# Staging of weights in a two-block fp32-accurate kernel: host-packed units of one transfer each, issued by SyncE instead of ScalarE

## Chip, cores and metric

One Trainium2 chip, one core. The metric is device time in microseconds of one execution. A trace of one execution of the kernel before is read below; "PE" is TensorE, "DVE" VectorE, "ACT" ScalarE, "POOL" GpSimd, "SP" SyncE, and a "q" behind an engine's name (ACTq, SPq) is that engine's instruction queue, where transfers are issued.

## What is computed

Two blocks of layers on 512 tokens of 1,024 features, in float32. The first block has two layers, each with three mixers that run side by side (sparse attention over the top 128 keys, gated linear attention, a pooling mixer) and a feed-forward network with a short convolution. The second block has four layers (kinds A, B, C, A): grouped attention, neighbourhood attention, differential attention, with a context stream of 256 tokens beside the 512.

```python
x = first_block(x, positions, norm1_g, w_in, ..., w_out, norm2_g, w_up, conv_w, conv_b, w_down, final_norm_g)
...
h = rms_norm_2(x, norm_g[i]) * (1.0 + sc[:, None]) + sh[:, None]
u, z = jnp.split(h @ w_in, [n_mix_cols], axis=-1)
...
x = x + gt[:, None] * ((o * jax.nn.silu(z)) @ w_out)
```

What matters here is the products with weights: `w_in`, `w_out`, `w_up`, `w_down` in the first block and three pairs of `w_in`, `w_out` in the second, all float32 in HBM.

## The kernel before, in words

Every weight goes through a staging unit. `wsplit` (L303) takes a tile `wst` of 128 x 1024 float32 (four buffers), begins its transfers on ScalarE's queue (L311), and makes two float16 halves of 256 times the weight: `whi`, the rounded value, by ScalarE (L322, or L318 and L319 in the first block's mixers), and `wlo`, the rest, by VectorE (L323) or GpSimd (L320). `whi` and `wlo` have four buffers each. TensorE then does three products for each block of 128 rows (L338 to L340 and L1564 to L1566). A buffer of `wst` is free again when `wlo` has been made, so up to four units are staged and four are split ahead of TensorE.

The transfers read the weights as they lie in HBM: a unit of eight row blocks by 128 columns is one transfer whose rows are 512 bytes long; a pair unit of the second block (`pair_job`, L1547) is two such transfers, one for each chunk of columns; a unit of `early1` and `late1` is two transfers of 1 KB rows; a unit of an output matrix of the second block is one transfer of 2 KB rows. The first unit of each mixer layer (`unit` with parts, L761) holds three narrow pieces of 16, 4 and 64 columns: VectorE clears the tile and three transfers fill it.

SyncE's queue has the other transfers: the input `xin` (L246), the modulation weights `ast` (L414), copies of heads between partitions (`put_q`, `put_k`, L606 to L615; `swap_heads`, L1149), and all transposing transfers: `pt<-hl` (L669, the exponentials of an attention item turned for the product with the values), `qs`, `kh`, `kl` (L1625, L1641) and `og<-ohl` (L1763).

```python
for src, at, m, *k in parts:
    getattr(nc, ("scalar","sync","sync")[0]).dma_start(sv[:, slice(*k), at:at + m] if k else sv[:, :, at:at + m],
                                 src.rearrange("(k p) c -> p k c", p=128))
```

The order of the work is set twice. The program writes pieces of work out by a count of TensorE time (`tick`, L185), with attention, modulation and the mixers as channels beside the products. Then a scheduler sets the order of the instructions on each engine by a simulated time line (the last lines of the file). Each engine works through its own order; an instruction that waits holds what stands behind it.

Of the kernel before, what the change touches and what calls it, by code (L numbers as in the profile page):

```python
# [21 lines left out]
KD = 8  # L22
# [17 lines left out]
# ---------------------------------------------------------------- host layout  # L40
# [5 lines left out]
def constants():  # L46
# [15 lines left out]
    # first block rope: rows of a pair of heads  # L62
# [11 lines left out]
    # second block rope  # L74
# [8 lines left out]
    # window mask of the neighbourhood: query (m2, r, c8), key column (m4, c8')  # L83
# [11 lines left out]

def layout(inp):
    """Only slices, transposes, pads and copies of the inputs, and constants of the shapes."""
# [3 lines left out]
    for k in ("w_in", "w_out", "w_up", "w_down", "ada_w_2", "a_w_in_2", "a_w_out_2",  # L101
              "b_w_in_2", "b_w_out_2", "c_w_in_2", "c_w_out_2"):
        o[k] = a[k]
# [33 lines left out]
    # relative position bias: [query (m2, r, c8), head, 6 blocks of 8 columns, 8 rows, 8]  # L137
# [15 lines left out]
LAT0, LAT1, CTX, LAT = range(4)    # streams: halves of the latent tokens, the context, all latent tokens  # L153


# ---------------------------------------------------------------- the kernel
class Kern:
    def __init__(self, tc, I, out, dbg=None, stop=None):
        self.tc, self.nc, self.I, self.out = tc, tc.nc, I, out
        self.dbg = dbg or {}  # L160
        self.stop = stop
        self.waiting = []
        self.chan = []
        self.pipe = []
        self.late = []
        self.ready = set()
        self.nw, self.share = 0, (0,)
        with ExitStack() as es:
            self.es = es
            self.main()  # L170
# [62 lines left out]
        # the second block's context stream takes the place of the mixers' outputs  # L233
# [38 lines left out]
    # ---- helpers  # L272
# [26 lines left out]
    def wunit(self, src, c0, r0=0, nk=KD, ncol=128, sc=None):  # L299
        """Rows r0.., nk blocks of 128, and ncol columns of a weight, as hi and lo halves of 256 w."""  # L300
        return self.wsplit([(src[r0:r0 + 128 * nk, c0:c0 + ncol], 0, ncol)], nk, ncol, sc)

    def wsplit(self, parts, nk, ncol, sc=None, clear=False):  # L303
# [23 lines left out]
    def mm_fm(self, ps, units, c0, hh, hl, t0, t1, order=None):  # L327
        """psum[m, t] = sum over K of W[K, c0:c0+128] h[K, t]; a generator of pieces."""
# [19 lines left out]
    def mm_tm(self, ps, unit, hh, hl, t0, t1):  # L348
        """psum[token, tile, 128] = h[K, token] W[K, 128]; a generator of pieces."""
# [13 lines left out]
    def rsq(self, a, shape, name):  # L363
        """a ** -0.5 by Newton's steps; a is a small tile."""
# [5 lines left out]
    def setup(self):  # L370
# [18 lines left out]
        # conditioning: silu of both vectors, and every layer's modulation [feature, chunk, lat / ctx]  # L389
# [5 lines left out]
        # each vector's hi and lo parts  # L395
# [10 lines left out]
    def ada(self):  # L406
        """Modulation: 512 columns of one layer's weight, two chunks of rows at a time."""
# [56 lines left out]
    def means(self, accs, then):  # L464
        """then(mean squares + eps [token, tile of each of accs])."""
# [19 lines left out]
    def bcast(self, y, n4, ps):  # L485
        """psum[:, token] = GK * y[token] on every partition."""
# [14 lines left out]
    # ---- first block: the products take x g, and rstd scales their results  # L501
# [5 lines left out]
    def rstd1(self, acc, ms=None):  # L507
        """rt [token, tile] and rb [any, token]: rstd / 256."""
# [21 lines left out]
    def start(self, xin, sq):  # L530
        """x to [feature, token], the products' operand and rstd."""
# [70 lines left out]
    def put_q(self, y, qs, n):  # L602
        """Stack the hi and lo halves of a pair of heads on the partitions."""
# [5 lines left out]
    def put_k(self, y, kh, kl, n, hs=((0, 0), (1, 64))):  # L609
        """Both halves of the partitions hold each head's hi, and its lo part."""  # L610
# [50 lines left out]
    def spread(self, p, w):  # L661
        """Keys on the partitions: hi halves, then lo halves."""
# [17 lines left out]
    def slot(self, then=None, skew=3):  # L680
        """One step of the pipeline: what has waited, then the oldest item's second half if there are enough."""
# [13 lines left out]
    # ---- first block  # L695
    def early1(self, w):
        """x += W h for the mixers' chunks that are there first."""
        nc = self.nc
        h = [[m[:, c] for c in (0,1,6,7)] for m in self.mx]
        for o in range(0, KD, 2):  # L700
            c = slice(128 * o, 128 * o + 256)
            u = self.wsplit([(w[256 * (k // 2):256 * (k // 2) + 256, c], 0, 256, n, n + 2)
                             for n, k in enumerate((0,1,6,7)) if n % 2 == 0], 4, 256)
# [6 lines left out]
    def late1(self, w):  # L710
        """The other chunks' products."""
        h = [[m[:, c] for c in range(KD) if c not in (0,1,6,7)] for m in self.mx]
        rows = [c for c in range(KD) if c not in (0,1,6,7)]
        for o in range(0, KD, 2):
            c = slice(128 * o, 128 * o + 256)
            u = self.wsplit([(w[128 * k:128 * k + 256, c], 0, 256, n, n + 2)
                             for n, k in enumerate(rows) if n % 2 == 0], 4, 256)
# [3 lines left out]
    def down1(self, w):  # L721
        """The second matrix of the feed forward network."""
        for o in range(KD):
            yield [self.wunit(w, 128 * o, 128 * k, n) for k, n in ((0, 8), (8, 8), (16, 6))], 0, self.gg, None
# [23 lines left out]
    def mixers1(self, l):  # L748
        nc, I = self.nc, self.I
        win = I["w_in"][l]  # L750
# [6 lines left out]
        # rotation tables of this layer: times rstd / 256  # L757
# [3 lines left out]
        def unit(c0, done, parts=None):  # L761
            if parts:
                u = self.wsplit(parts, KD, 128, clear=True)
            else:
                u = self.wunit(win, c0)
# [5 lines left out]
        def tunit(c0, done):  # L771
            u = self.wunit(win, c0)
# [1146 lines left out]
```

## Time and profile before

| | us |
|---|---|
| median of 3 runs | 2996.72 |
| lowest and highest run | 2987.07, 3007.28 |
| profiled execution, span from first to last instruction | 3000.3 |
| TensorE busy in it | 2645.7 (88%) |
| mean granted clock of TensorE | 0.958 |

The list of times does not say which run was profiled; what lies around the span is not shown apart. The span stands 3.6 us (0.1%) above the median and inside the spread of the runs. Stages by time: first block's layer 0 mixers to about 230 us, its network to 680, layer 1 mixers to 900, its network to 1350, then the four layers of the second block to the end.

### The profile page before, as it was taken

How to read it: one execution, taken by the hardware profiler on the slowest of the kernel's cores; microseconds unless marked ns; L12 is line 12 of the kernel's file. 1: busy time of each engine (PE TensorE's matmuls, PEld its weight loads, DVE VectorE, ACT ScalarE, POOL GpSimd, SP SyncE). 2: the span in 40 equal slices, each digit the busy share in tenths (PEclk: the TensorE clock that was granted, in tenths of full speed). 3: DMA queues.
4: the chain of work that ended last, by engine and by line, in shares of the span. 5: the costliest groups of instructions: out<-in, count | busy, mean ns of one | idle time of the engine just before them, and what ended most of it. 6: DMA issues, size and time to landing. Idle time of an engine off the chain costs nothing.

```text
span 3000.3 us, 59334 instructions
## 1 busy us (share of the span) xinstructions
PE 2645.7 (88%) x22591; PEld 1767.0 (59%) x22604; DVE 2119.0 (71%) x4157; ACT 1664.9 (55%) x3471; POOL 1512.3 (50%) x1341
## 2 busy tenths in 40 slices
PE   6889999998889899998888898898888898978886
PEld 3554444445554444457666587777667676757664
DVE  5966877536857877346787865666769877886875
ACT  6475555335665655334666655645546555555764
POOL 5763222126753422137665756656555545346764
PEclk8999999999999999999999999999999999989998
DMA  5356566333355565325787647766525546525985
GB/s 143 97 113 144 176 200 184 99 104 96 94 113 168 172 203 153 102 76 117 147 152 143 140 96 148 149 139 128 110 74 110 114 102 115 103 50 126 173 149 112
DMA packets 913647, 384.91 MB, mean 128 GB/s; under 512 B 572638, under 2 KB 877584, under 8 KB 913360
## 3 DMA queue, kind: packets, MB, share of 16 engines
q1 hardware_dynamic: 595232, 205.35, 34.4%
q10 hardware_dynamic: 317008, 172.88, 20.8%
q8 instruction: 177, 2.90, 0.4%
q0 software_dynamic: 1120, 2.88, 0.4%
q14 instruction: 110, 0.90, 0.1%
HBM read 232.35 MB, written 2.10 MB: 78 GB/s over the span
## 4 chain that ended last, share of the span: by engine, by line
PE 32%; DVE 27%; DMA 13%; issue 10%; ACT 9%; POOL 7%; SPq 1%; ACTq 1%; POOLq 0%; DVEq 0%
DMA pt<-hl 8%; PE pj L338 5%; PE pj L339 5%; PE pj L340 5%; DVE wlo L323 3%; PE pj L1564 3%; PE pj L1566 3%; PE pj L1565 3%; DVE mx L639 3%; POOL hl L666 2%; DMA ast<-i_ada_w 2%; ACT P L648 2%; ACT whi L322 2%; DVE nm L645 2%; DVE alo L419 1%
## 5 line engine op out<-in xcount | busy, mean ns | idle before, releaser
L666 POOL TENSOR_TENSOR hl<-P,hl 128x768 f16<-128x768 f32 (+4 forms) x368 | 466.1, 1274 | 333.0 <-ACT hl L665 271.6
L323 DVE SCALAR_TENSOR_TENSOR wlo<-wst,whi 128x1024 f16<-128x1024 f32 (+1 forms) x292 | 375.6, 1287 | 211.2 <-ACT whi L322 210.3
L1564 PE MATMUL pj<-whi,hh 128*128 128x256 f16 x1664 | 457.0, 275 | 20.0 <-DVE sz L1743 13.3
L1565 PE MATMUL pj<-wlo,hh 128*128 128x256 f16 x1664 | 456.8, 275 | 0.0
L1566 PE MATMUL pj<-whi,hl 128*128 128x256 f16 x1664 | 455.8, 275 | 0.7 <-POOL hl L1401 0.4
L322 ACT ACTIVATE whi<-wst 128x1024 f16<-128x1024 f32 (+1 forms) x292 | 304.3, 1043 | 245.2 <-PE pj L339 164.8
L339 PEld LDWEIGHTS <-whi 128*128 128x128 f16 x1936 | 192.4, 99 | 228.5 <-issue 54.3
L648 ACT ACTIVATE P<-S,nm,rq 128x768 f32<-128x768 f32 (+1 forms) x256 | 225.7, 883 | 171.8 <-DVE nm L645 114.7
L338 PEld LDWEIGHTS <-whi 128*128 128x128 f16 x1936 | 192.5, 100 | 198.2 <-issue 18.6
L340 PEld LDWEIGHTS <-wlo 128*128 128x128 f16 x1936 | 192.3, 99 | 196.7 <-issue 7.3
L639 DVE TENSOR_REDUCE mx<-S 128x1 f32<-128x768 f32 (+4 forms) x352 | 250.4, 719 | 78.2 <-PE S L631 59.7
L665 ACT CAST hl<-P 128x768 f16<-128x768 f32 (+4 forms) x368 | 230.3, 637 | 103.8 <-DMA pt<-hl 68.4
L676 PE MATMUL O<-vh,pt 128*128 128x64 f16 (+1 forms) x1472 | 196.1, 202 | 93.1 <-DMA pt<-hl 85.0
L630 PE MATMUL S<-kh,qs 128*128 128x256 f16 (+3 forms) x672 | 209.3, 318 | 63.4 <-ACT P L648 54.2
L676 PEld LDWEIGHTS <-pt 128*128 128x128 f16 x1536 | 147.2, 101 | 132.4 <-DMA pt<-hl 123.8
L1564 PE MATMUL pj<-whi,mxl 128*128 128x256 f16 x704 | 196.4, 279 | 18.1 <-DVE sz L1743 10.6
L631 PE MATMUL S<-kl,qs 128*128 128x256 f16 (+3 forms) x672 | 200.1, 319 | 0.0
L1565 PE MATMUL pj<-wlo,mxl 128*128 128x256 f16 x704 | 196.2, 279 | 2.0 <-DVE wlo L323 2.0
L1566 PE MATMUL pj<-whi,mxl 128*128 128x256 f16 x704 | 195.0, 279 | 1.1 <-DVE mxl L1404 1.1
L677 PE MATMUL O<-vl,pt 128*128 128x64 f16 (+1 forms) x1472 | 195.3, 202 | 0.0
L678 PE MATMUL O<-vh,pt 128*128 128x64 f16 (+1 forms) x1472 | 195.0, 202 | 0.0
L338 PE MATMUL pj<-og,whi 128*128 128x256 f16 (+1 forms) x512 | 164.7, 325 | 32.9 <-DVE mxh L1539 15.1
(403 smaller groups left out, 7817.5 us busy)
## 6 DMA issues: line engine op xcount, KB each, us to landing
ast<-i_ada_w SPq DMA_DIRECT2D x96, 512.0 KB
wst<-i_w_up ACTq DMA_DIRECT2D x88, 512.0 KB
wst<-i_w_in ACTq DMA_DIRECT2D x44, 512.0 KB
wst<-i_a_w_in ACTq DMA_DIRECT2D x80, 256.0 KB
wst<-i_w_down ACTq DMA_DIRECT2D x32, 512.0 KB
wst<-i_b_w_in ACTq DMA_DIRECT2D x64, 256.0 KB
wst<-i_c_w_in ACTq DMA_DIRECT2D x64, 256.0 KB
wst<-i_w_out ACTq DMA_DIRECT2D x32, 256.0 KB
```

Source lines behind the costliest of these rows:

```text
L322: nc.scalar.activation(hi[:, :n], st[:, :n], AF.Copy, scale=s)
L323: nc.vector.scalar_tensor_tensor(lo[:, :n], st[:, :n], s, hi[:, :n], op0=OP.mult, op1=OP.subtract)
L338: nc.tensor.matmul(ps, a, u, start=(k == 0), stop=False)
L339: nc.tensor.matmul(ps, a, v, start=False, stop=False)
L340: nc.tensor.matmul(ps, b, u, start=False, stop=(k == kt - 1))
L639: nc.vector.reduce_max(mx, s[:, :w], axis=AX.X)
L648: nc.scalar.activation(p[:, :w], s[:, :w], AF.Exp, bias=nm, scale=scale, accum_out=su)
L666: nc.gpsimd.tensor_tensor(hl[:, w:2 * w], p[:, :w], hl[:, :w], op=OP.subtract)
L676: nc.tensor.matmul(o, pt[:, i], vh, start=(i == 0), stop=False)
L1564: nc.tensor.matmul(d, hh[:, k, s], hi[:, k % 4], start=(k == 0), stop=False)
L1565: nc.tensor.matmul(d, hh[:, k, s], lo[:, k % 4], start=False, stop=False)
L1566: nc.tensor.matmul(d, hl[:, k, s], hi[:, k % 4], start=False, stop=(k == KD - 1))
```

## The change

The host lays every unit out as it will lie in `wst`: one array `wts` of 334 units, each 128 rows of 1,024 float32, contiguous. `weight_units` yields them in one fixed list; `wunit` looks a unit up by its key and begins one transfer, on SyncE. `wsplit` and its clearing of the tile are gone, and the callers name keys instead of slices. The bytes are the same, but for the narrow units, which now carry their zeros. All that splits the halves and multiplies is as it was. The line numbers shift (L311 becomes L362, L669 becomes L719, L1149 becomes L1189).

```diff
+def weight_units(a=None):
...
+        w = A["w_up"][l] if a else None
+        for k in range(KF):
+            for c0 in (128 * k, DFF + 128 * k):
+                yield of(("up", l, c0), lambda: stack([rows(w, 128 * j, c0, 128) for j in range(8)]))
...
+    wts = [np.pad(u.reshape(128, -1), ((0, 0), (0, 1024 - u[0].size))) for _, u in weight_units(a)]
+    o["wts"] = np.stack(wts)
...
-    def wsplit(self, parts, nk, ncol, sc=None, clear=False):
+    def wunit(self, *key, nk=KD, ncol=128, sc=None):
+
         nc = self.nc
         st = self.wst.tile([128, 1024], F32, name="wst")
         n = nk * ncol
-        sv = st[:, :n].rearrange("p (k c) -> p k c", k=nk)
-        if clear:
-            nc.vector.memset(st[:, :n], 0.0)
-        for src, at, m, *k in parts:
-            getattr(nc, ("scalar","sync","sync")[0]).dma_start(sv[:, slice(*k), at:at + m] if k else sv[:, :, at:at + m],
-                                         src.rearrange("(k p) c -> p k c", p=128))
+        nc.sync.dma_start(st[:, :n], self.I["wts"][self.wat[key]][:, :n])
...
         def unit():
-            return [self.wsplit([(win[512 * e:512 * e + 512, c:c + 128], 128 * n, 128) for n, c in enumerate((c0, c1))],
-                                4, 256) for e in range(2)]
+            return [self.wunit("min", i, c0, e, nk=4, ncol=256) for e in range(2)]
```

How the order moves is shown at three places. First, ScalarE at the start of the program, before (`identf`, `small` and `vec` are constants, `xsq` the squares of the input, `x<-S` and `x<-pj` its transposed copies):

```order
L545 ACTIVATE xsq,ms<-xin_87 128x1024
L311 DMA wst<-i_w_in 128x8x16
L311 DMA wst<-i_w_in 128x8x4
L541 COPY x<-S 128x4x128
L311 DMA wst<-i_w_in 128x8x64
L393 ACTIVATE cth<-cc 128x16
L545 ACTIVATE xsq,ms<-xin_88 128x1024
L311 DMA wst<-i_w_in 128x8x128 x2
L541 COPY x<-pj 128x4x128
L311 DMA wst<-i_w_in 128x8x128
```

The same place after:

```order
L595 ACTIVATE xsq,ms<-xin_87 128x1024
L591 COPY x<-S 128x4x128
L595 ACTIVATE xsq,ms<-xin_88 128x1024
L443 ACTIVATE cth<-cc 128x16
L591 COPY x<-pj 128x4x128
L595 ACTIVATE xsq,ms<-xin_89 128x1024
```

The six transfers between the first four instructions on the input are gone from ScalarE; nine units now stand on SyncE right behind the four of `xin`.

Second, SyncE in layer 0 of the first block, where the heads of the gated linear attention are swapped between partitions (`vx` values, `gr` gate), before:

```order
L607 DMA qi<-h 64x512 x2
L1149 DMA vx<-vb 32x4x64 x7
L1149 DMA gr<-grt 32x4x64 x8
L1149 DMA vx<-vb 32x4x64 x8
L1149 DMA gr<-grt 32x4x64 x8
L1149 DMA vx<-vb 32x4x64
L614 DMA kh<-h 64x512
```

The same place after:

```order
L657 DMA qi<-h 64x512 x2
L362 DMA wst<-i_wts 128x1024 x2
L1189 DMA vx<-vb 32x4x64 x7
L1189 DMA gr<-grt 32x4x64 x8
L1189 DMA vx<-vb 32x4x64 x8
L1189 DMA gr<-grt 32x4x64 x8
L1189 DMA vx<-vb 32x4x64
L362 DMA wst<-i_wts 128x1024 x7
L664 DMA kh<-h 64x512
```

Seven units, the 15th to the 21st, now stand behind all 32 copies; in the kernel before, ScalarE issued them whenever a buffer was free.

Third, SyncE in the first layer of the second block, an attention of kind A, before:

```order
L1763 DMA_TRANSPOSE og<-ohl 128x2x128 x2
L669 DMA_TRANSPOSE pt<-hl 128x12x128 x3
L1763 DMA_TRANSPOSE og<-ohl 128x2x128 x2
L1625 DMA_TRANSPOSE qs<-qst 128x12x128
L669 DMA_TRANSPOSE pt<-hl 128x12x128 x2
L669 DMA_TRANSPOSE pt<-hl 128x4x128 x4
```

The like place after:

```order
L1800 DMA_TRANSPOSE og<-ohl 128x2x128
L362 DMA wst<-i_wts 128x1024
L719 DMA_TRANSPOSE pt<-hl 128x12x128
L1800 DMA_TRANSPOSE og<-ohl 128x2x128
L362 DMA wst<-i_wts 128x1024
L719 DMA_TRANSPOSE pt<-hl 128x12x128
L1800 DMA_TRANSPOSE og<-ohl 128x2x128
L1662 DMA_TRANSPOSE qs<-qst 128x12x128
```

Units stand between the transposes, singly or by twos, so that some `pt<-hl` come right behind one.

## Rows read from the trace of the kernel before

**Rows 1.** The page: busy time; the chain that ended last, by engine.
```profile
PE 2645.7 (88%) x22591; PEld 1767.0 (59%) x22604; DVE 2119.0 (71%) x4157; ACT 1664.9 (55%) x3471; POOL 1512.3 (50%) x1341
...
PE 32%; DVE 27%; DMA 13%; issue 10%; ACT 9%; POOL 7%; SPq 1%; ACTq 1%; POOLq 0%; DVEq 0%
```

**Rows 2.** The chain by line, from 1350 us to 3000 us.
```profile
by line: DMA pt<-hl 11.8%; issue 10.0%; PE pj L1564 4.8%; PE pj L1566 4.8%; PE pj L1565 4.7%; DVE mx L639 4.5%; ACT P L648 3.2%; POOL hl L666 3.1%; DVE nm L645 3.0%; DVE wlo L323 2.8%; PE pj L338 2.2%; PE pj L339 2.1%; POOL qny L367 2.1%; P
```

**Rows 3.** Waits: engine line waited for: us in total, times, longest us.
```profile
DVE wlo L323 <- ACT whi L322: 211.5, 119, 6.3
PEld L676 <- DMA pt<-hl: 123.8, 109, 4.0
PE O L676 <- DMA pt<-hl: 92.9, 87, 3.8
ACT wst L318 <- DMA wst<-i_w_in: 45.2, 25, 3.9
```

**Rows 4.** Issues on ACTq, line 311: ns min/median/max, first and last start us.
```profile
L311 ACTq DMA_DIRECT2D wst<-i_w_up x88: 374/374/375, 249.6 to 1168.3; - x88
L311 ACTq DMA_DIRECT2D wst<-i_a_w_in x80: 374/381/1144, 1289.4 to 2843.4; - x80
L311 ACTq DMA_DIRECT2D wst<-i_b_w_in x64: 374/400/1103, 1625.8 to 2033.4; - x64
L311 ACTq DMA_DIRECT2D wst<-i_c_w_in x64: 374/378/1577, 2102.6 to 2515.6; - x64
```

**Rows 5.** Time line of ACT, 0 to 75 us: start us, us, instruction [idle before].
```profile
4.48 1.06 ACT L545 ACTIVATE xsq<-xin 128x1024 f32<-128x1024 f32 x1 [1.04 <-DMA xin<-i_x]
...
5.84 5.05 ACTq L311 DMA_DIRECT2D wst<-i_w_in  x1
10.94 0.21 ACT L393 ACTIVATE cth<-cc 128x16 f32<-128x16 f32 x1 [4.53 <-issue]
...
65.74 1.06 ACT L318 ACTIVATE wst<-wst 128x1024 f32<-128x1024 f32 x1 [1.93 <-DMA wst<-i_w_in]
66.24 0.37 ACTq L311 DMA_DIRECT2D wst<-i_w_in  x1
66.84 0.60 ACT L831 ACTIVATE f<-S 128x512 f32<-128x512 f32 x1
```

**Rows 6.** The chain by line, 0 to 75 us.
```profile
by line: issue 16.2%; PE pj L340 13.2%; PE pj L338 12.9%; PE pj L339 12.5%; ACTq L311 7.2%; POOL wlo L320 6.2%; DMA wst<-i_w_in 6.2%; DMA identf<-i_identf 5.2%; DVE sc L832 2.3%; PE pz L974 2.1%; POOL qb L864 1.7%; POOL lny L367 1.6%; ACT x
```

**Rows 7.** The chain in order of time, its longest pieces: start us, us, what.
```profile
66.24 4.62 DMA wst<-i_w_in
211.12 3.76 DMA wst<-i_w_out
...
708.64 4.37 DMA wst<-i_w_in
```

**Rows 8.** The input's transfers (128 rows of 4 KB each), line 246: ns min/median/max.
```profile
L246 SPq DMA_DIRECT2D xin<-i_x x4: 397/420/622, 0.7 to 2.1; - x4
```

**Rows 9.** DMA queues: packets, MB, share of 16 engines (q1 is SyncE's, q10 ScalarE's).
```profile
q1 hardware_dynamic: 595232, 205.35, 34.4%
q10 hardware_dynamic: 317008, 172.88, 20.8%
```

**Rows 10.** Windows: stretch, length, PE, PEld, DVE, ACT, POOL busy, PEclk, DMA share, GB/s.
```profile
2.50:4.50 2.00, 0.00 (x0) 0.00 (x0) 0.00 (x0) 0.96 (x2) 1.67 (x4) 1.00 0.95 361
600.00:675.00 75.00, 75.00 (x355) 33.93 (x353) 26.87 (x26) 29.52 (x35) 17.69 (x13) 1.00 0.39 104
1350.00:3000.00 1650.00, 1407.97 (x13933) 1119.20 (x13931) 1208.51 (x2661) 944.98 (x2268) 975.57 (x915) 0.95 0.62 123
```

**Rows 11.** Transposes on SPq, line 669: ns min/median/max, first and last start us.
```profile
L669 SPq DMA_TRANSPOSE pt<-hl x368: 1167/1286/2994, 161.2 to 2970.5; - x184
```

**Rows 12.** Time lines of ACTq, SPq and PE around the swap of heads in layer 0.
```profile
85.24 0.37 ACTq L311 DMA_DIRECT2D wst<-i_w_in  x1
...
105.93 0.58 SPq L1149 DMA_DIRECT2D vx<-vb  x1
...
126.93 0.38 PE L338 MATMUL pj<-hh,whi 128*128 128x512 f16 x1
```

**Rows 13.** The splitting of a unit in this stage: ns min/median/max.
```profile
L318 ACT ACTIVATE wst<-wst x34: 1038/1057/1062, 21.6 to 741.4; 128x1024 f32<-128x1024 f32 x34
L319 ACT CAST whi<-wst x34: 1027/1042/1057, 25.4 to 755.3; 128x1024 f16<-128x1024 f32 x34
L320 POOL TENSOR_TENSOR wlo<-wst,whi x34: 2108/2132/2586, 26.5 to 761.0; 128x1024 f16<-128x1024 f32 x34
```

More of the change, by code (lines that the diff above doesn't have):

```diff
@@ L93, in constants, with rows, stack, of @@
     return c
+def weight_units(a=None):
+    def rows(w, r, c0, n):
+        return w[r:r + 128, c0:c0 + n]
+    def stack(parts):
+        return np.stack(parts, 1)
+    def of(key, make):
+        return key, (make() if a is not None else None)
+    A = a or {}
+    for l in range(2):
+        w = A["w_in"][l] if a else None
+        def misc(w=w):
+            z = np.zeros((128, 8, 128), np.float32)
+            for at, c, n in ((0, C_GL, 16), (32, C_WI, 4), (64, C_KI, 64)):
+                for k in range(8):
+                    z[:, k, at:at + n] = rows(w, 128 * k, c, n)
+            return z
+        yield of(("misc", l), misc)
+        for c0 in ([C_QI + 128 * c for c in range(2)] + [C_QB, C_KB, C_VB, C_RB, C_VB + 128, C_RB + 128, C_UC, C_UC + 128]
+                   + [b + 128 * c for c in range(4) for b in (C_KA, C_QA, C_VA)]):
+            yield of(("in", l, c0), lambda: stack([rows(w, 128 * k, c0, 128) for k in range(8)]))
+        w = A["w_out"][l] if a else None
+        for what, ks in (("early", (0, 1, 6, 7)), ("late", (2, 3, 4, 5))):
+            for o in range(0, KD, 2):
+                yield of((what, l, o), lambda: stack([rows(w, 128 * k, 128 * o, 256) for k in ks]))
+        w = A["w_up"][l] if a else None
+        for k in range(KF):
+            for c0 in (128 * k, DFF + 128 * k):
+                yield of(("up", l, c0), lambda: stack([rows(w, 128 * j, c0, 128) for j in range(8)]))
+        w = A["w_down"][l] if a else None
+        for o in range(KD):
+            for k, n in ((0, 8), (8, 8), (16, 6)):
+                yield of(("down", l, o, k), lambda: stack([rows(w, 128 * (k + j), 128 * o, 128) for j in range(n)]))
+    for i in range(4):
+        kind, j = i % 3, i // 3
+        w = A["abc"[kind] + "_w_in_2"][j] if a else None
+        pairs = [(1024 + 128 * c, 1280 + 128 * c) for c in range(2)] if kind == 0 else []
+        for g in range(8):
+            if kind:
+                pairs.append((1024 + 128 * g, 2048 + 128 * g))
+            pairs.append((128 * g, (1536 if kind == 0 else 3072) + 128 * g))
+        for c0, c1 in pairs:
+            for e in range(2):
+                yield of(("min", i, c0, e), lambda: np.concatenate(
+                    [stack([rows(w, 512 * e + 128 * k, c, 128) for k in range(4)]) for c in (c0, c1)], 2))
+        w = A["abc"[kind] + "_w_out_2"][j] if a else None
+        for p in range(4):
+            for n in range(2):
+                yield of(("mout", i, p, n), lambda: stack([rows(w, 256 * p + 128 * k, 512 * n, 512) for k in range(2)]))
@@ L167, in __init__ @@
         self.nw, self.share = 0, (0,)
+        self.wat = {key: n for n, (key, _) in enumerate(weight_units())}
         with ExitStack() as es:
@@ L708, in early1, with late1, down1 @@
                 nc.vector.scalar_tensor_tensor(self.x[:, o + n], ps, WI, self.x[:, o + n], op0=OP.mult, op1=OP.add)
[L710 removed]
+    def late1(self, l):
         h = [[m[:, c] for c in range(KD) if c not in (0,1,6,7)] for m in self.mx]
[L713 removed]
         for o in range(0, KD, 2):
[L715 to L717 removed]
+            u = self.wunit("late", l, o, nk=4, ncol=256)
             for n in range(2):
                 yield [u], 128 * n, h, (2,3,0,1)
[L721 removed]
+    def down1(self, l):
         for o in range(KD):
[L724 removed]
+            yield [self.wunit("down", l, o, k, nk=n) for k, n in ((0, 8), (8, 8), (16, 6))], 0, self.gg, None
     def proj_out1(self, products, accs, g, hn):
@@ L759, in mixers1, with unit @@
         self.rsr = pm.tile([128, S], F32, name="rsr")
[L761 to L765, printed above, removed]
+        def unit(c0, done):
+            u = self.wunit("misc", l) if c0 is None else self.wunit("in", l, c0)
             ps = self.psA()
@@ L771, in tunit @@
         def tunit(c0, done):
-            u = self.wunit(win, c0)
+            u = self.wunit("in", l, c0)
             ps = self.psA()
@@ L807, in put_misc @@
             self.after(4.0, tr)
-        self.run(unit(0, put_misc, [(win[:, C_GL:C_GL + 16], 0, 16), (win[:, C_WI:C_WI + 4], 32, 4),
-                                    (win[:, C_KI:C_KI + 64], 64, 64)]))
+        self.run(unit(None, put_misc))
         for c in range(2):
@@ L959, in mixers1 @@
             self.tick(1.2)
-        self.run(self.early1(I["w_out"][l]))
+        self.run(self.early1(l))
         while ca in self.chan or cg in self.chan or cp in self.chan:
@@ L1521, in out_pair @@
             self.tick(1.0)
-        us = [self.wunit(wout, 512 * n, 256 * p, 2, 512, self.wsub) for n in range(2)]
+        us = [self.wunit("mout", i, p, n, nk=2, ncol=512, sc=self.wsub) for n in range(2)]
         og = [[self.og[2 * p + k][n] for k in range(2)] for n in range(2)]
@@ L1646, in put_v, with kv_job @@
         nc.vector.scalar_tensor_tensor(vl, ps, WI, vh, op0=OP.mult, op1=OP.subtract)
-    def kv_job(self, kind, win, c, cv, kh, kl, vh, vl, st, after=None):
+    def kv_job(self, kind, i, c, cv, kh, kl, vh, vl, st, after=None):
         def then(u, y):
@@ L1663, in done, with a_keys @@
                 after()
-        return self.pair_job(win, c, cv, done)
-    def a_keys(self, win):
+        return self.pair_job(i, c, done)
+    def a_keys(self, i):
         pl = self.pl
@@ L1714, in after @@
                     nc.sync.dma_start(st["rp"], self.I["rpb"][:, 2 * g:2 * g + 2])
-            jobs.append(self.kv_job(kind, win, 1024 + 128 * g, 2048 + 128 * g, kh, kl, vh, vl, st, after))
+            jobs.append(self.kv_job(kind, i, 1024 + 128 * g, 2048 + 128 * g, kh, kl, vh, vl, st, after))
         if kind == 1:
```

47 lines of the change are left out of this document (19 added, 28 removed).

## Prediction

> **What bounds the kernel now.** I read the page first: TensorE is busy 2645.7 us of the 3000.3, 88%, and no other engine over 71% [rows 1]. So 354.6 us without TensorE is the most that better feeding could give, apart from the clock. Then the chain that ended last, by engine: TensorE 32%, VectorE 27%, transfers 13%, ScalarE 9%, but the two queues that this change trades between only 1% each, ACTq and SPq [rows 1]. The reader is to see there that a transfer's issue is hardly ever what the end waits for. Then the second block alone, 1350 to 3000 us: its chain has 11.8% in the transposing transfers `pt<-hl` and no weight transfer among its first lines [rows 2]. The list of waits says the same from TensorE's side: it waits 87 and 109 times, at the product and at its weight load, for `pt<-hl`, 92.9 and 123.8 us; the one large wait for a staged weight is ScalarE's in the first block's mixers, 45.2 us in 25 times [rows 3]. So weights are mostly staged long before they are used, and what is scarce is the turned exponentials. The change puts the weights into the very queue that issues them.
>
> **Part 1: issues leave ScalarE.** 458 issues of some 0.38 us (374 to 400 ns at the median, [rows 4]) are 174 us of ScalarE's queue. They mostly cost nothing, because the queue runs ahead of the engine: at 66.24 us an issue of 0.37 us lies inside an activation that runs from 65.74 to 66.80, and the next one starts at 66.84 [rows 5]. One does cost: the third narrow piece of the first unit holds the queue for 5.05 us, and ScalarE is idle for 4.53 us behind it [rows 5], on the chain: ACTq L311 has 7.2% of the first 75 us, 5.4 us [rows 6]. That is the lower bound, 5.4 us. The upper one is the whole ACTq share, which prints as 1% and so is at most 1.5%, 45 us [rows 1]. I take 15 us, the 0.5% that a printed 1% is at least, since it is nearest to the row that I can see. The two clearings by VectorE that go are not on the chain where I read it; I cost them at nothing, covered at the start by the wait for the input.
>
> **Part 2: one transfer of 4 KB rows in place of 512-byte rows.** ScalarE's queue moved 172.88 MB in 20.8% of 16 engines' span [rows 9], that is 0.208 x 3000.3 x 0.524 / 172.88 = 1.89 us of all engines for a unit of 0.524 MB. The input's four transfers have the new shape exactly, and in the 2 us in which they run alone the engines move 361 GB/s at a share of 0.95 [rows 10], 380 GB/s when busy: 1.38 us for a unit. So 0.51 us is saved, 334 times, 170 us of transfer time. What of it lies on the path?
> - Landing of a weight: the longest pieces of the chain hold three weight transfers, 4.62, 3.76 and 4.37 us, 12.75 us in all [rows 7]. The first `xin`, issued at about 0.7 us [rows 8], is used at 4.48 [rows 5]: 3.8 us with three others behind it. About 0.8 us less for each of the first and the last: I take 3 us, between 0 and 12.75.
> - Room for the transposes: the second block has 136 units (80 + 64 + 64 pair transfers by two, and 32 of output matrices), so 136 x 0.51 = 69 us less transfer time beside them, with the engines 62% busy there [rows 10]. The bounds are 0 and 69 us; I weigh it by the 11.8% of the chain that lies in `pt<-hl` [rows 2], 8 us.
>
> The Trainium skill, "DMA: Bandwidth & Descriptors", section "Specifications", puts the least size for line rate at 512 bytes, which would leave nothing to win by longer rows. The rows disagree: 172.88 MB in 20.8% is 17.3 GB/s for each of 16 engines, the input's rows reach 23.8 [rows 9, 10]. By that rule the 8 us would be 0, and the sum below 2,991.
>
> **Part 3: 334 issues on SyncE.** An issue of the new shape takes 0.42 us [rows 8], so SyncE gets 140 us more, 57 us of it in the second block, between transposes of 1.29 us each [rows 11]. Weighed by the same 11.8%, 7 us. A transpose behind a unit also finds 1.38 us of transfer ahead of it: 136 x 1.38 x 0.118 = 22 us if none of that was paid before. It was paid in part, since both queues already shared the engines, so the cost lies between 0 and 29 us, and I take 12.
>
> What stands behind a waiting unit? In layer 0, seven units now stand behind the swaps of heads. The first of them, issued at 85.24 us before, would go out after 105.93 [rows 12]. With 4.62 us to land [rows 7] and 1.06 + 1.04 + 2.13 us to split [rows 13] it is ready at 115.4, and TensorE needs it (its fm product, L338) at 126.93 [rows 12]. The eleven us of cover make it free; without the cover it would cost up to 21 us, twice, since layer 1 has the same code. The other way round, a unit that waits for its buffer holds the transposes behind it; that is the rival below. I put it at nothing in the sum, because the scheduler gave the unit that place by its own reckoning of when the buffer is free.
>
> **The sum.** -15 - 3 - 8 + 12 = -14 us on the profiled execution's span of 3000.3. That span is 3.6 us above the median of the runs shown, so the same 14 us on the median, 2996.7, give 2,983 us. A measurement tells about 1% of this kernel, 30 us, from no change. So I forecast no change that can be told. The scheduler also deals the order anew on all five engines, as the three places show; the runs of one order alone spread from 2987 to 3007, and I allow a new order as much again to either side.
>
> **Rivals.**
> - *Both reliefs reach the end (faster).* In the second block ScalarE loses 240 issues of 0.38 us, 91 us, and the transfers 69 us. For it: ScalarE's work on the exponentials lies in the chain (ACT P L648 3.2%, [rows 2]), and TensorE waits for `pt<-hl` almost 200 times. Against it: the issue inside an activation, and only 1% of ACTq. If half of the 160 reaches the end, 80 us, and with it the 5 of the start and the 3 of the landings, the median comes to 2,909; if a quarter, to 2,949. Chance 0.35 for more than 1%.
> - *The queue holds the transposes (slower).* Of 368 `pt<-hl`, TensorE waits for 196, 0.53 of them [rows 3, 11]. If a unit in front of one waits for its buffer, the hold is how far `wlo` comes later than reckoned; the nearest row is VectorE's wait for `whi`, 211.5 us in 119 times, 1.8 us [rows 3]. 136 units x 0.53 x 1.8 = 130 us, less the 26 that the other terms give: 3,101. If half of the units have a transpose right behind them, 65 - 26 = 39 us: 3,036. It decides from a mean hold of 26 / (136 x 0.53) = 0.36 us on. For it: the third place of the order. Against it: the units are staged four deep, so in a settled stretch a buffer has long been free when its turn comes. Chance 0.18 for more than 1%.
>
> The Trainium skill, "DMA: Bandwidth & Descriptors", section "Queues, rings and completion order", says that an engine consumes one queue's descriptors in ring order and goes round between queues by packets. By that rule a transpose waits for the whole unit ahead of it, but never shares with one behind it: the 22 us above against what is saved where the unit comes second. No row here shows the order inside a queue.
>
> **How the numbers follow.** No change within 1%: 0.47, with 2,983. Faster by over 1%: 0.35; slower by over 1%: 0.18. The range reaches from 2,920, which leaves out the end of the fast rival, to 3,036, the half-priced slow one. The likeliest case's own range is 2,967 to 3,010.
>
> **What would show it.** Right: ACTq gone from the chain and ScalarE's idle 4.53 us at the start gone; the transfers' share for the weights down from 20.8% to about 15% on a queue with as many bytes more; `pt<-hl` still near 11.8% of the second block's chain; TensorE's waits for it within some 20% of 92.9 and 123.8 us. Wrong: new waits of SyncE for `wlo` with transposes behind them and TensorE's waits for `pt<-hl` half as long again (the slow rival); or these waits and VectorE's and ScalarE's shares of the chain down by a quarter with TensorE above 91% (the fast one). If the first products come 15 us later in layer 0, the cover in part 3 was false.

## The result and the profile after

The changed kernel takes 2949.13 us (median of 4 runs, 2944.55 to 2951.45), beside 2999.14 for the kernel before on the same chip: a ratio of 0.9838, with a 95% interval of 0.9818 to 0.9858. That is 1.6% faster, 48 to 50 us, more than the 1% that the forecast took for no change. The forecast was no change, 2983 us with 2967 to 3010 as its own range; the time lies below that, inside the wide range of 2920 to 3036, and on the fast rival's quarter, 2949.

The page of the changed kernel, the rows that answer to [rows 1] and [rows 9] (busy time; share of 16 engines' span; the chain by engine):

```profile
PE 2633.1 (89%) x22604; PEld 1760.3 (60%) x22604; DVE 2126.6 (72%) x4155; ACT 1665.8 (57%) x3471; POOL 1530.8 (52%) x1341
...
q1 hardware_dynamic: 643328, 378.39, 53.4%
...
q10 hardware_dynamic: 432, 0.20, 0.0%
...
PE 35%; DVE 24%; DMA 12%; issue 10%; ACT 9%; POOL 9%; SPq 0%; ACTq 0%; DVEq 0%; POOLq 0%
```

The span is 2947.3 us. TensorE does the same work in it, so its share rises by one point only. The two queues took 34.4% + 20.8% = 55.2% of 3000.3 us before, 1656 us of all engines, and now 53.4% of 2947.3, 1574 us: 82 us of transfer time are gone, where the prediction reckoned with 334 x 0.51 = 170.

The chain by line in the second block, as [rows 2], here from 1324 us on:

```profile
by line: issue 13.1%; DMA pt<-hl 8.6%; PE pj L1601 4.1%; DVE mx L689 4.1%; PE pj L1603 4.0%; PE pj L1602 4.0%; POOL hl L716 3.8%; POOL qny L417 3.5%; ACT P L698 3.3%; DVE wlo L373 2.7%; DMA qs<-qst 2.6%; DVE nm L695 2.4%; PE pj L388 2.0%; P
```

And the waits that answer to [rows 3], with SyncE's own over the whole run (us in total, times, longest):

```profile
PEld L726 <- DMA pt<-hl: 88.0, 90, 3.5
PE O L726 <- DMA pt<-hl: 60.4, 69, 3.2
ACT wst L368 <- DMA wst<-i_wts: 45.8, 21, 8.6
...
SPq L362 <- DVE wlo L373: 670.5, 175, 15.7
SPq L719 <- POOL hl L716: 299.2, 167, 7.6
```

In the kernel before, SyncE's first row was this one:

```profile
SPq L669 <- POOL hl L666: 442.6, 173, 13.5
```

In the second block alone, where 304 of the 368 transposes stand, SyncE's rows are these, before and then after:

```profile
SPq L669 <- POOL hl L666: 336.4, 133, 13.5
```

```profile
SPq L719 <- POOL hl L716: 238.4, 130, 7.6
SPq L362 <- DVE wlo L373: 125.8, 33, 15.7
```

The reader is to see three things. First, TensorE's rows for the turned exponentials `pt` fall, and so does their share of the chain, from 11.8% to 8.6%. The two rows may not be added: every wait of the product for `pt` (87 before, 69 after) overlaps one of the weight load, since both wait for the same transpose. Counted once, TensorE waited 124 us before and 88 after. Second, SyncE now waits 670.5 us in 175 units for `wlo`, which frees a buffer, but only 125.8 us of that, in 33 of 136 units, lies in the second block; the rest lies in the first, with its 64 transposes. Third, SyncE still stands ready when the exponentials' low half `hl` comes about as often as before, 130 times of 304 against 133, with less time to spare. So the hold that the slow rival feared is there, but mostly where few transposes are. From the instruction records I added up how long each of the 304 transposes of the second block was issued after its `hl` was done: 189 us in all before, 162 after. (That fall comes with the rows and not with the queue, as the orders below show: packed units on ScalarE have 152 to 167 us, on SyncE 162 to 181.)

The start, as [rows 5], ScalarE's time line:

```profile
4.70 1.06 ACT L595 ACTIVATE xsq<-xin 128x1024 f32<-128x1024 f32 x1 [1.26 <-DMA xin<-i_x]
...
7.75 0.22 ACT L443 ACTIVATE cth<-cc 128x16 f32<-128x16 f32 x1
...
9.53 1.06 ACT L595 ACTIVATE xsq<-xin 128x1024 f32<-128x1024 f32 x1 [1.09 <-DMA xin<-i_x]
```

The issue of 5.05 us and the idle 4.53 us behind it are gone. To see where the 50 us came from I compared, in both traces, when the k-th unit has been split: 6 us earlier at the first unit, 14 at the end of layer 0's network, 25 at the end of layer 1's mixers, 27 at the end of the first block, 38 after mixer B, 46 to 53 around the end of mixer C, 50 at the last unit. Half came in the first block, almost all of it in the start and the mixers, and half in the second.

### The profile page after: what moved, and what is told of

It reads as the page before. It is cut to its first block, busy times and chain, and to the rows that moved or that the text cites. A ratio compares the mean times of both kernels' runs of the same rounds, so it can differ in the third digit from the quotient of the medians.

```text
span 2947.3 us, 59391 instructions
## 1 busy us (share of the span) xinstructions
PE 2633.1 (89%) x22604; PEld 1760.3 (60%) x22604; DVE 2126.6 (72%) x4155; ACT 1665.8 (57%) x3471; POOL 1530.8 (52%) x1341
## 3 DMA queue, kind: packets, MB, share of 16 engines
q1 hardware_dynamic: 643328, 378.39, 53.4%
## 4 chain that ended last, share of the span: by engine, by line
PE 35%; DVE 24%; DMA 12%; issue 10%; ACT 9%; POOL 9%; SPq 0%; ACTq 0%; DVEq 0%; POOLq 0%
DMA pt<-hl 6%; PE pj L388 5%; PE pj L389 5%; PE pj L390 5%; DVE wlo L373 3%; PE pj L1601 2%; PE pj L1603 2%; PE pj L1602 2%; DVE mx L689 2%; POOL hl L716 2%; ACT P L698 2%; DMA ast<-i_ada_w 2%; POOL qny L417 2%; ACT whi L372 2%; DMA qs<-qst 1%
## 5 line engine op out<-in xcount | busy, mean ns | idle before, releaser
L716 POOL TENSOR_TENSOR hl<-P,hl 128x768 f16<-128x768 f32 (+4 forms) x368 | 474.0, 1294 | 319.8 <-ACT hl L715 257.2
```

Of the source, the lines that this page charges most:

```text
L716: nc.gpsimd.tensor_tensor(hl[:, w:2 * w], p[:, :w], hl[:, :w], op=OP.subtract)
```

## The experiments

Sixteen kernels, each timed in three rounds beside the kernel before. The theory to be tested: long rows shorten the transposes' way, and ScalarE is freed. The rivals: SyncE's shared queue matters rather than ScalarE's time; or the scheduler dealt a good order.

**Packed units, ScalarE issues.** One word changed in the changed kernel.

```diff
-        nc.sync.dma_start(st[:, :n], self.I["wts"][self.wat[key]][:, :n])
+        nc.scalar.dma_start(st[:, :n], self.I["wts"][self.wat[key]][:, :n])
```

> The changed kernel, its packed units issued by ScalarE again (one transfer of long rows each, 334 issues). Rows theory (the gain comes from transfer time freed beside the transposes): it keeps most of the gain, 2945 to 2962 us. Issuer theory (the gain comes from ScalarE's queue, which no longer waits for the splits and issues nothing): it loses most of it, 2975 to 3000, with only the start's 6 us kept because the narrow pieces are gone. Order theory (the gain comes from the order that the scheduler dealt): its order differs from both others, so anything from 2940 to 3000, and ScalarE's own waits would not explain it.

Measured: 2971.91, ratio 0.9914 (0.989 to 0.9938). Somewhat more than half of the gain is there without SyncE. Its queue and its issues (ns min/median/max, first and last start, as [rows 4]):

```profile
q10 hardware_dynamic: 48528, 173.23, 18.9%
...
L362 ACTq DMA_DIRECT2D wst<-i_wts x334: 334/334/452, 4.6 to 2866.4; - x167
```

The same bytes in rows of 4 KB take 18.9% of 2974.1 us, 562 us against 624 before: 1.70 us for a unit of 0.524 MB, not the 1.38 of the input's rows. And no issue holds the queue for longer than 0.45 us.

**The changed kernel's order, short rows.** The host lays a unit out by row blocks; one transfer reads it in rows of 512 bytes, 1 KB or 2 KB. All else, every engine's order included, is the changed kernel's.

```diff
-        nc.sync.dma_start(st[:, :n], self.I["wts"][self.wat[key]][:, :n])
+        m = chunk(key)
+        src = self.I["wts"][self.wat[key]].rearrange("a b -> (a b)")[:128 * n]
+        nc.sync.dma_start(st[:, :n].rearrange("p (k c) -> p k c", c=m), src.rearrange("(k p c) -> p k c", p=128, c=m))
```

> The changed kernel in the changed kernel's own order of instructions on every engine, one transfer for each unit on SyncE, but stored so that its rows are as short as before (512 bytes, 1 KB, 2 KB). Rows theory: the gain goes, 2975 to 3000 us, and TensorE's waits for the turned exponentials return to some 90 and 120 us. Issuer theory and order theory: it stays within 0.3% of the changed kernel, 2942 to 2958.

Measured: 2970.0, ratio 0.9902 (0.9874 to 0.9931). The rows alone are worth 21 us by the medians, 19 by the ratios. At the start SyncE is held as ScalarE was before, here for the first four units, and beside it the changed kernel:

```profile
3.27 9.96 SPq L368 DMA_DIRECT2D wst<-i_wts  x4
```

```profile
2.83 3.59 SPq L362 DMA_DIRECT2D wst<-i_wts  x4
```

**The kernel before, its 458 transfers on SyncE.** `nc.sync` in place of the first entry of L311's choice.

> The kernel before, its 458 transfers unchanged but issued by SyncE. Rows theory: no gain, 2985 to 3010. Issuer theory: ScalarE is relieved as in the changed kernel, so it has most of the gain, 2950 to 2970, less what 124 more issues cost SyncE. Order theory: its order is nearer to the changed kernel's than to the one before, so 2945 to 2975 as well; it is told from the issuer theory by the nudged orders.

Measured: 2961.73, ratio 0.9875 (0.985 to 0.99). Moving the short transfers as they are gives 37 us in the order that comes out, though the second block's transposes are issued later: 207 us behind their `hl` in sum, against 189 before.

**The changed kernel with 66 small clearings.** The program has VectorE clear a 128 x 64 tile, which nothing reads, at every fifth unit; in the trace all 66 run in the first 33.5 us.

> The changed kernel with a clearing of 128 x 64 by VectorE at every fifth unit (66 of them, about 0.1 us each), which only makes the scheduler deal another order from some point on. Order theory: the time moves by more than the 7 us that the clearings can take, either way by up to 30 us. Rows and issuer theory: 2945 to 2960.

Measured: 2960.79, ratio 0.9877 (0.9854 to 0.9899), 12 us above the changed kernel. The clearings take 7.4 us of VectorE (66 at 112 ns), and the units are 3.5 us late at the end of the first block and 9 at the end of mixer C, so the order has a share of its own.

**Only the narrow first units packed, in the kernel before.**

```diff
-                u = self.wsplit(parts, KD, 128, clear=True)
+                u = self.wsplit(None, KD, 128, whole=I["misc"][l])
```

> The kernel before, in which only the first unit of each mixer layer is changed: it comes as one packed transfer of 4 KB rows in place of a clearing and three narrow pieces; all other units as before, on ScalarE. Theory: of the 50 us of the change, what the start shows in the traces (its first split unit comes 5.9 us earlier after the change) is due to this edit alone: about 2993 us (2990 to 2996), with ScalarE's idle 4.5 us and its 5.05 us issue gone at the start and all units of the first block some 6 us earlier. Rival, order: the edit also reorders a tenth as many of TensorE's instructions as the change does (2,512 rows against 22,681), and that alone moves the time by more than the 6 us, either way. Rival, absorbed: the end stays at 2999 because the units behind are held by something else.

Measured: 2986.02, ratio 0.9969 (0.9954 to 0.9983): 9 to 10 us, more than the 3 to 9 expected. The first unit is split 3 us earlier than before, the 37th 5 us, the last of the first block 11 us; so the start itself gave 3 to 5, and what the rest owes to layer 1's packed unit and to the new order isn't told apart. And the hold did not go:

```profile
8.02 4.53 ACTq L315 DMA_DIRECT2D wst<-i_w_in  x1
...
12.59 0.59 ACT L545 COPY x<-pj 128x512 f32<-128x512 f32 x1 [3.45 <-issue]
```

It is now the third of the ordinary units that holds ScalarE (in its time line). So the narrow piece was not the reason. Both holds came at the third transfer of 1,024 rows (before: the third in all; here: the fourth, behind one of 128 rows), and the kernel with short rows on SyncE has its own; the change's units of 128 rows have none at the start. This fits a queue that takes only so many rows at a time; no run measures how many.

**One more tiny transfer per unit on ScalarE, waiting for nothing.**

```diff
+        nc.scalar.dma_start(self.dum[0:1, self.nw % 16:self.nw % 16 + 1], self.I["identf"][0:1, 0:1])
```

> The changed kernel with one more transfer for each of the 334 units, of a single element, issued by ScalarE and waiting for nothing of the unit; SyncE issues the units as after the change. It puts the issue time back on ScalarE (334 x 0.37 = 124 us of its queue) without the wait for a free buffer. Measured so far: after 2949, packed units issued by ScalarE 2972. Theory of issue time: the 23 us between those two are issue time, so 2965 to 2975. Rival, hold: they come from issues that wait for wlo and hold ScalarE's activations behind them, so this stays at 2949 to 2956. Rival, order: the extra instruction deals the order anew (8,166 rows on TensorE) and the time moves by about 10 us, which alone would give 2945 to 2962.

Measured: 2965.18, ratio 0.9906 (0.9886 to 0.9925). As the theory of issue time wanted, but it does not bear it out:

```profile
L364 ACTq DMA_DIRECT2D dum<-i_identf x334: 229/238/612, 4.6 to 314.5; - x167
```

All 334 were issued in the first 315 us, 80 us of ScalarE's queue in one stage, and there the time was lost: in the profiled run, at 2971.79 the slowest of the four, the 37th unit is split 21 us later than after the change, the last one 26. It suggests that issues cost when they crowd ScalarE in a mixer stage, beside whatever the new order costs, and does not say what they cost spread out.

**The same, but waiting for the `wlo` of four units earlier.** This puts the whole of it back on ScalarE: issue and hold.

```diff
+        if len(self.los) == 4:
+            nc.scalar.dma_start(self.dum[0:1, self.nw % 16:self.nw % 16 + 1], self.los[0][0:1, 0:1])
```

> The changed kernel with one more transfer for each unit from the fifth on, of a single element, issued by ScalarE and reading the low half wlo of the unit four places earlier: it waits on ScalarE for exactly what freed the staging buffer, as the unit's own transfer did in the kernel before. Theory of the hold: 2965 to 2980, with waits of ScalarE's activations put down to wlo that the changed kernel hasn't, and at least 10 us above the run with the transfers that wait for nothing. Theory of issue time: the same as that run, 2965 to 2975, and the two within 5 us. Order alone (25,014 rows on TensorE): 2940 to 2960 by chance.

Measured: 2930.11, ratio 0.9784 (0.9761 to 0.9807): 19 us faster than the changed kernel, the opposite of what both theories of ScalarE wanted. Its waits and extra issues:

```profile
PEld L731 <- DMA pt<-hl: 91.7, 95, 3.4
...
PE O L731 <- DMA pt<-hl: 65.7, 74, 3.1
...
L363 ACTq DMA_DIRECT2D dum<-wlo x330: 569/570/1184, 22.8 to 2823.9; - x165
```

330 x 0.57 = 188 us of ScalarE's queue, spread over the whole program, and no loss.

**The same in another order.** TensorE time of a product counted 2% longer when the pieces are written out.

> The run with the transfers of one element on ScalarE that wait for wlo (2930 us, 19 below the changed kernel, where the theory of the hold wanted 2965 to 2980), in another order: TensorE time of a product counted 2% longer (25,425 of TensorE's rows differ). If a hold on ScalarE is of use by itself, since it lets exponentials through later or weights later, this stays at 2925 to 2938. If 2930 was a lucky order, this lies at 2940 to 2965.

Measured: 2959.33, ratio 0.9859 (0.9835 to 0.9883). This lies in the range for a lucky order, 2940 to 2965. With four orders of the change itself between 2949 and 2973 (below), a hold on ScalarE costs nothing that these two orders show, and that it gains anything isn't shown either.

**The kernel before in another order,** counted 2% shorter.

> The kernel before, with the TensorE time of a product counted 2% shorter when the program writes out its pieces: the same instructions and transfers, dealt in another order (8,624 of TensorE's rows differ). It sizes what order alone does. If order alone is worth what I allowed, 10 us to either side, it lies between 2989 and 3009 and mostly not at 2999; if it is worth the 23 us that packing and row length leave unexplained, beyond that; if the order hardly matters, 2996 to 3002.

Measured: 2999.05, ratio 1.001 (0.9998 to 1.0022). This order, a fifth of TensorE's rows moved, changed nothing.

**Packed units issued by GpSimd.**

> The changed kernel with its packed units issued by GpSimd: a third queue, so the units share a queue neither with ScalarE nor with the transposes. Up to here TensorE's waits for pt<-hl (the rows of its weight load and its product together) are 148 to 160 us in the four runs with packed units on SyncE, with or without one more issue per unit on ScalarE, and 183 with packed units on ScalarE; short rows add 26 to 34 us to either. Theory of the shared queue: what lowers these waits is that units and transposes stand in one queue, so here they are 175 to 195 us as with ScalarE's queue, and the time is 2965 to 2985. Rival, ScalarE: what lowers them is ScalarE freed of the issues, so here 145 to 165, and the time 2945 to 2960 unless GpSimd's own issues, in front of its products of the exponentials, cost more than that; in that case the waits still tell.

Measured: 3054.41, ratio 1.0172 (1.0144 to 1.0199). The theory of the queue wanted 2965 to 2985 and misses the time; the rows of the waits, 120.2 + 91.4 = 211.6 us, lie above its 175 to 195. By these the run can't decide, because GpSimd makes the exponentials' low halves, and there the hold that I had feared on SyncE appears (waits; GpSimd's issues):

```profile
POOL wst L362 <- DVE wlo L373: 388.9, 133, 8.7
...
L362 POOL DMA_DIRECT2D wst<-i_wts x334: 527/591/644, 4.2 to 2943.6; - x167
```

**Short rows in the second block alone,** in the changed kernel's order.

> The changed kernel's own order of instructions; rows of 512 bytes and 2 KB as in the kernel before in the second block alone, packed 4 KB rows in the first. With short rows in both blocks it was 2970, with long rows 2949. The prediction put 3 us of the longer rows into landings of weights and 8 us into room for transposes in the second block. Theory from the two traces: about 16 of the 21 us come in the first block's two mixer stages, where ScalarE waits for its weights, and about 5 in the second block: 2952 to 2957 here. Rival, as the prediction had it: most of it in the second block, 2962 to 2968.

Measured: 2961.91, ratio 0.9869 (0.9847 to 0.9891): 13 us by the medians, 9 by the ratios, of the 21 (19). My reading of two traces, 5 us here and 16 in the first block, missed its range of 2952 to 2957. By subtraction 8 to 10 are left for the first block, but in the trace with short rows everywhere its last unit is 16 us late; the shares of the two blocks do not add up, so the first block's is known only as 8 to 16. The rows of the waits for `pt` are those of short rows everywhere (102.5 and 72.0):

```profile
PEld L734 <- DMA pt<-hl: 101.0, 102, 3.3
PE O L734 <- DMA pt<-hl: 71.3, 73, 3.0
```

**Four more orders.** The changed kernel counted 2% longer and 2% shorter, and the packed units on ScalarE likewise.

> The changed kernel in another order: TensorE time of a product counted 2% longer (15,507 of TensorE's rows differ), same instructions and transfers. With the run that was nudged by small clearings (2961) it sizes the order's own share. If the 48 us of the change were its queue and its rows, 2940 to 2965, with TensorE's waits for pt<-hl at 145 to 165 us; if they were a lucky order, 2965 to 2990.

> The changed kernel with TensorE time of a product counted 2% shorter: 11,182 of TensorE's rows differ. Theory of the queue: 2945 to 2965. Theory of order: anywhere from 2945 to 2980.

> Packed units issued by ScalarE (2972 in its own order), TensorE time of a product counted 2% longer: 4,967 of TensorE's rows differ. Theory of the queue: still 2965 to 2985, above all runs with SyncE issuing but 2973. Theory of order: spread as wide as SyncE's runs, 2945 to 2980.

> The same with the time counted 2% shorter: 6,716 of TensorE's rows differ. Theory of the queue: 2965 to 2985. Theory of order: 2945 to 2980, and on the other side of SyncE's mean of 2961 than the other run as often as not.

Measured: SyncE 2973.45 (ratio 0.9917, 0.9888 to 0.9946) and 2951.78 (0.985, 0.9825 to 0.9875); ScalarE 2979.08 (0.9937, 0.9915 to 0.9959) and 2976.57 (0.9927, 0.9898 to 0.9955). The first of these lies above the range of the theory it was to test, 2940 to 2965, and inside the one for a lucky order; its units are level with the change's to the end of the first block, 11 us late at the end of mixer C and 22 at the last.

**Short rows in the order of 2973.**

> The order of the changed kernel with the time counted 2% longer (2973 with long rows), instruction by instruction, with the short rows of the kernel before in every unit. If the rows are worth what they were in the changed kernel's order, 21 us, 2990 to 2998; if that was half the order's, 2980 to 2988; if the prediction's 11 us (landings 3, room 8) hold in this order, 2984.

Measured: 2990.59, ratio 0.9968 (0.9951 to 0.9984). The rows are worth 17 us (15 by the ratios) in a second order too.

Together, in medians, one order to an entry:

| | short rows | packed rows |
|---|---|---|
| ScalarE issues | 2996 to 3000 (before), 2999; first units packed 2986 | 2972, 2977, 2979 |
| SyncE issues | 2962, 2970, 2991 | 2949 (the change), 2952, 2961, 2973 |
| SyncE, and tiny transfers on ScalarE | | 2930, 2959, 2965 |

## Why the prediction was wrong

By ratios, against about 2998 us: packing the first units gives 9 us (0.9969). Packing the rest on ScalarE leads to 0.9926, the mean of three orders, 13 more. Issuing on SyncE leads to 0.9871, the mean of four, 17 more. The change's own order stands at 0.9838, 10 below that mean. The four make 49 us. The means are over few orders: the four on SyncE differ by up to 24 us, so the 17 and the 10 would move with another draw.

**What bounds the kernel: right in the main.** The chain had `pt<-hl`, and that is what fell. No single wait took its place; `issue` in the second block's chain rose to 13.1%. But these waits alone do not rank the orders: counted once, they are 107 us in the order of 2952, 97 in that of 2973, and 100 with short rows in the order of 2991. And one reading was wrong: the 87 and 109 waits are not 196 but 109, of 0.30 of the transposes and not 0.53, because the rows of product and weight load hold the same waits.

**Part 1, 15 us: 9 of it found, the reason failed.** The run with the first units packed gave 9 us, of which 3 to 5 show at the start, about the 5.4 on the chain; the reason I named, a narrow third piece, was wrong, since the hold moved to another transfer. The rest of the 15, ScalarE's issues on the path, I could not find: 188 us of issues put back on ScalarE cost nothing in two orders (2930 and 2959, where the change without them has 2949 to 2973). The run with 2965 suggests that they cost when crowded.

**Part 2, 3 + 8 us: mis-sized by nearly half.** The same order with short and with long rows differs by 21 and 17 us in medians, 19 and 15 by the ratios. The term for the second block, 8 us, measured 9 to 13; the term for the landings, 3 us, stands against 8 to 16 for all of the first block. Two steps were off in opposite directions. A unit does not cost 1.38 us but 1.70 on ScalarE's queue, because the input's rows were read in a stretch where they ran alone; so 0.19 us are saved a unit there, not 0.51. And the weight of 11.8% for what reaches the end was too small: with the units on SyncE 82 us of transfer time are gone, 0.25 us for each of 334 units, 33 for the second block's 136, and 9 to 13 of these came out at the end, a quarter to two fifths.

**Part 3, +12 us: the step that failed, and with the wrong sign.** Instead of 12 us lost, the move gave 17 as a mean over orders, where the 10 of ScalarE's issues and these 12 together wanted a loss of 2.

The cost that I charged exists, but it is small. I charged all 136 units; after the change only 48 of the 304 transposes stand right behind a unit. These are issued 0.21 us after their `hl`, 10 us in sum, the other 256 after 0.59 us: most units fall where no transpose is ready, since SyncE waits for `hl` at nearly half of the transposes. Behind a unit a transpose of 12 blocks takes 3.78 us from issue to last packet against 3.45 for the others, one of 8 blocks 3.58 against 2.86: 0.3 to 0.7 us, not 1.38, and 18 us in sum, before any weighing for what reaches the end. For all 304 together the time from `hl` to issue is 152 to 167 us in the three orders with packed units on ScalarE and 162 to 181 in the four on SyncE, 10 us more as a mean.

What I left out is a gain, and it is in the DMA packets, which I counted between the first and the last packet of each transpose. In the kernel before, 23 of the 160 with 12 blocks had over 40 weight packets inside and took 4.13 us from issue to last packet, against 3.48 for the others; with packed units on ScalarE 6 had, at 5.54 against 3.53 us; after the change none. Long packets and short ones aren't alike in such a count: the change's order with short rows still has 16 with over 40 of 512 bytes, at 4.13 us. In bytes, the 240 transposes with 12 or 8 blocks had 6.6 MB of weights inside before, 7.3 with packed units on ScalarE, 10.4 with GpSimd's queue, 2.2 after the change and at most 2.5 in its order with short rows. Their time from issue to last packet adds up to 827 to 834 us in all six kernels with ScalarE issuing, whatever the rows, and to 798 to 816 in all eight with SyncE issuing and no tiny transfers. So two queues share the engines within a transpose far more than one queue does.

This is the round between queues, by packets, that the prediction named from the Trainium skill ("DMA: Bandwidth & Descriptors", "Queues, rings and completion order"), and the bytes agree with it.

That this accounts for all of the 17 us is not shown. Counted once, TensorE's waits for `pt` are 101 to 107 us in the three orders with packed units on ScalarE and 88 to 107 in the four on SyncE, some 7 us less as a mean; where the other 10 come from stays open. ScalarE's freed queue is the rival for them, and only the tiny transfers speak against it. One of SyncE's four orders, 2973, reaches ScalarE's three, and the time of the run with a third queue was spoilt by GpSimd's holds.

**The seven units behind the swaps in layer 0: right.** They went out from 99 us on, and TensorE waits for none of them: between 85 and 170 us its longest waits are for the pooling and linear attention, 4.8 and 5.3 us. The first products were not late.

**The order: allowed for, too narrowly.** I allowed the spread of the runs, 10 us to either side. Seven orders with packed units on SyncE lie between 2930 and 2973. The change drew one 10 us better than the mean of its four, which is luck.

**The rivals.** The fast one was right in its time (2949), by luck, and half right in its mechanism: transfer time reaches the end, ScalarE's 91 us do not. The slow one was wrong: its hold is in the trace, but of the 670.5 us only 125.8 fall in the second block, and the transposes right behind a unit are issued 0.21 us after their `hl`, where the rival reckoned with 1.8 us for half of 136. Of the marks that I had set, ACTq gone from the chain and the idle 4.53 us gone came true; `pt` near 11.8% and waits within 20% failed (8.6%; 29% and 35% less), and the weights' share fell only by some 2 points of the two queues' 55.2, not 6.

## What to carry to other kernels

Before charging an issue to an engine's queue, look at how often that queue is already waiting when its important instruction comes ready; units put into such slack cost little even when they wait themselves. Look where the waits lie before reading a total: four fifths of SyncE's long wait lay where few transposes were. The price of a transfer is read where it runs in company, not alone. A large reordering by a scheduler is a draw: time a few neighbouring orders with the same transfers before crediting a change with the last 10 us, since here four orders of the same transfers spread over 24.

## What the hardware showed that I had not expected

- A queue can hold its engine at an issue while its earlier transfers are under way. Three or four transfers of 1,024 rows in a row did it at the start (5.05, 4.53 and, on SyncE, 4 issues in 9.96 us); 334 transfers of 128 rows did not once on ScalarE (at most 0.45 us).
- A transpose has fewer bytes of weights inside it when the weights stand in its own queue (2.2 MB in 240 transposes) than when they stand in another (6.6 and 7.3 MB on ScalarE's, 10.4 on GpSimd's), and is over sooner: 798 to 816 us against 827 to 834 in sum.
- Rows of 512 bytes (some of 1 and 2 KB) and of 4 KB differ by 10% in engine time when other traffic is there (624 against 562 us for all weights), much less than the input's rows alone suggest, and still by 15 to 21 us at the end.
- TensorE's full clock came earlier with the earlier start. The granted clock of the first two windows of 25 us, before and then after the change (length, busy times, PEclk, DMA share, GB/s):

```profile
0.00:25.00 25.00, 7.34 (x37) 6.16 (x38) 15.12 (x40) 16.34 (x26) 6.88 (x15) 0.74 0.75 206
25.00:50.00 25.00, 22.27 (x87) 9.16 (x85) 11.59 (x12) 16.51 (x21) 18.45 (x10) 0.78 0.43 111
```

```profile
0.00:25.00 25.00, 8.62 (x37) 6.56 (x38) 16.10 (x39) 19.61 (x29) 9.93 (x16) 0.83 0.64 228
25.00:50.00 25.00, 25.00 (x111) 11.46 (x110) 12.90 (x15) 16.42 (x22) 22.96 (x13) 0.90 0.43 127
```

A mean of 0.78 between the levels of 1.2 and 2.4 GHz is 0.44 of the window at the lower one, 11 us, and 0.90 is 5 us. The run with only the first units packed, whose first unit is split 3 us earlier, has 0.76 and 0.90 in these windows. So a start that is earlier by 3 us may be worth about twice that, an estimate: 6 us less at half the clock are 3 us of work. No run separates the two.
